# mLSTM value products turned round: values stationary, weights passing, transposed back one projection later

## The chip, the cores and the metric

The kernel runs on one core of a Trainium2 chip. The metric is the device time of one execution in microseconds (us), taken as the median of several runs. The core has these engines: PE (TensorE: matmuls, and PEld for its weight loads), DVE (VectorE), ACT (ScalarE), POOL (GpSimd) and SP (SyncE, which issues nearly all DMA transfers here). Each engine works through its own queue in order. PE writes its results to PSUM, in 8 banks of 128 partitions x 512 fp32 numbers.

## The reference

Two layers, each with a mixer (four pairs of mLSTM heads beside eight heads of neighbourhood attention) and an MLP, over 1024 latent tokens and 256 context tokens; all of it in fp32. The change concerns the mLSTM alone. For one direction of one head, the reference computes, chunk by chunk:

```python
s = jnp.einsum('bhtd,bhsd->bhts', qc, kc) * w_intra
num = w_prev[..., None] * jnp.einsum('bhtd,bhde->bhte', qc, C) + jnp.einsum('bhts,bhse->bhte', s, vc)
qn = w_prev * jnp.einsum('bhtd,bhd->bht', qc, n) + jnp.sum(s, axis=-1)
h = num / jnp.maximum(jnp.abs(qn), jnp.exp(-m_t))[..., None]
...
C = w_c[..., None, None] * C + jnp.einsum('bhs,bhsd,bhse->bhde', w_s, kc, vc)
n = w_c[..., None] * n + jnp.einsum('bhs,bhsd->bhd', w_s, kc)
```

and of both directions' results `head_layernorm(hx_f + hx_b, norm_g) * jax.nn.sigmoid(o)`, where `head_layernorm` takes away the mean over the 64 channels of a head and divides by their spread. The kernel works in chunks of 128 tokens instead of 64, and it gets the sums `qn` and `n` as one more channel, whose value is 1 for every token.

## The kernel before

Tokens: T = 1280, in ten chunks of 128; a tile is two chunks (`u` = 0, 1), so there are five tiles `i`, the first of them the context. Heads go by pairs `pr` = 0 to 3 with `h` = 0, 1 in a pair; directions are `s` = 0, 1. `HD` = 64 channels a head.

`mlstm_out` (L540) is the mLSTM output stage of a layer. Its steps run over `seq`, 20 pairs (pr, i). A step projects a tile (`project_j`, L418: for each `u` eight k-tiles of 128 with three fp32r matmuls each, `mm3`, L85, that stand for one fp32 product by a split into high and low parts), 512 columns wide: keys and values of the next pair `pr + 1` (or, at the last pair, attention values), and queries and gate of this pair. In layer 1 the context has no output (`need_ctx` is false), so tile 0 projects 256 columns and has no output tile; 16 tiles are left there, 20 in layer 0.

- `kv_take` (L474) rotates the keys (`rope`, L431) into `kt`, copies the values to `va` (in the tile `kva`, 65 numbers a head, the last set to 1 by POOL), and leaves room for the turned keys `kT`.
- `kv_turn` (L493) transposes `kt` on PE and copies it to `kT` on ACT.
- `kv_state` (L500) weighs the values by token into `vw` on DVE (L517), multiplies them by `kt` (L519: head h to partitions h*64 to h*64 + 63 of the output) and adds to the running forward state `cst` (L526); the backward part waits in `kvb` for `kv_back` (L528).
- `mlstm_tile` (L592) is a generator in five stages: (1) load `gb`, the gate sums, by DMA; gate `og` on ACT; rotated queries `qr`; and the weights `wt` = exp(min(gb + tab, mask)) (L620 on DVE, L621 on ACT); (2) transpose `qr` (L625) into `qT` (L627); (3) scores and old-state products into four banks `sb` (L636, L637); (4) P = scores x wt on DVE (L647), value products with P stationary and `va` passing, for each u, h and s (L649), old state weighed into `hh` (L652) and the sum (L653); then the normaliser `den`, and the layer norm (L657 to L675); (5) transpose back to channels (L679), copy `yT` and store.

`mlstm_out` interleaves these stages by hand: a tile's transposes and scores come after the next tile's projection has been issued, its values after that. A list scheduler then sets the order of each engine's queue, with the program's order as priority. It moves matmuls across the stages where data are ready. `tc.issue_after(x)` (in use at L201, L852 and L1488) puts the instructions of a block behind instruction x on its engine.

`tick` (L59) draws a piece of side work: first `fill` (in layer 0 a part of the modulation on PE, `ada`), and when that has run out and its argument is true, one row of `ada_rows` (L185; on DVE L202, one DMA of 512 KB each; 16 rows in this stage of layer 0). `project_j` ticks with true; a tile ticks with true for i = 2 and 4 (L629).

Weights: `joint_weights` (L536) loads four chunks of 128x1024 for a pair through `split_chunk` (L71): DMA to `wraw` (two buffers), ACT copies the high part to `whi` (L81), DVE takes the low part `wlo` (L82); four buffers each. `kv_weights` (L447) does the same for the first pair's keys, values and the gates in three chunks, outside this stage; in layer 0 `opening` (L1512, its order written out by hand) does it.

PSUM: `BANKS`, two of tag `mm` for projections and six of tag `q` for the rest.

## Time and profile before

| what | us |
|---|---|
| median of 3 runs | 2876.28 |
| lowest and highest run | 2873.52, 2878.64 |
| the profiled execution, its own time | 2880.66 |
| span of the profiled execution | 2878.9 |

The rows of the profile are shown in the prediction, where they are used. In a row of the timeline stand the start in us, the length in us, the engine (PE, PEld, DVE, ACT, POOL, SP), the line of the kernel, the operation, output<-inputs by the program's names, the shape and the count. Matmuls overlap: what one costs PE is the distance to the next start. In a row of groups stand after the bar the busy time, the mean of one in ns, and the idle time of the engine just before, with what ended it. An fp32 product (not fp32r) shows as two matmul records, two passes; a transpose as one. 576 records of L649 stand for 36 tiles of 8 value products.

### The profile page before, as it was taken

Reading aid. Unit: us, or ns where it says so; the run is one execution under the profiler, and the core shown is the slowest. Engines: PE = TensorE matmul, PEld = TensorE weight load, DVE = VectorE, ACT = ScalarE, POOL = GpSimd, SP = SyncE. Lnnn points to the kernel's source line nnn. Section 1 sums busy time; section 2 is a strip of 40 time slices with the busy share of each in tenths; the row PEclk is TensorE's granted clock in tenths of the full one; section 3 lists DMA queues with packets and bytes.
Section 4 is the critical chain, followed back from the end, with each engine's and each line's share of the span. In section 5 each row is a group of like instructions: output and inputs, shape, how many; then the busy total and the mean of one; then the engine's idle time right before and its main releaser. Section 6 shows DMA issues by size and latency. Waiting matters only on the chain. (4 is left out here: it accounts for less than half of the span.)

```text
span 2878.9 us, 45683 instructions
## 1 busy us (share of the span) xinstructions
PE 2832.6 (98%) x16644; PEld 2409.0 (84%) x16644; DVE 2210.9 (77%) x5097; ACT 1263.5 (44%) x2426; POOL 67.2 (2%) x117
## 2 busy tenths in 40 slices
PE   8999999999999999999999999999999999999998
PEld 5888888889888888888889988888887788888888
DVE  7789987776798777599877778877785887759774
ACT  5333335564553333344554333335564533334453
POOL 0000000010000000000000000000010000000000
PEclk9999999999999999999999999999999999999999
DMA  7533333236446556798977122213346354478673
GB/s 249 165 115 105 112 120 107 90 121 201 152 163 227 191 191 205 276 324 289 319 254 256 67 89 71 75 64 116 110 143 194 130 191 142 155 255 311 210 255 100
DMA packets 278946, 497.42 MB, mean 173 GB/s; under 512 B 23328, under 2 KB 119584, under 8 KB 278720
## 3 DMA queue, kind: packets, MB, share of 16 engines
q1 hardware_dynamic: 278720, 494.49, 51.3%
q8 instruction: 131, 2.15, 0.3%
q14 instruction: 95, 0.78, 0.1%
HBM read 398.82 MB, written 95.59 MB: 172 GB/s over the span
## 5 line engine op out<-in xcount | busy, mean ns | idle before, releaser
L87 PE MATMUL q<-ah,whi 128*128 128x512 f32 (+1 forms) x1472 | 548.9, 373 | 2.5 <-ACT ah L997 1.9
L89 PE MATMUL q<-ah,wlo 128*128 128x512 f32 (+1 forms) x1472 | 547.9, 372 | 1.2 <-DVE wlo L998 1.1
L88 PE MATMUL q<-al,whi 128*128 128x512 f32 (+1 forms) x1472 | 548.4, 373 | 0.0
L87 PE MATMUL mm<-ah,whi 128*128 128x512 f32 (+1 forms) x1120 | 387.5, 346 | 1.5 <-ACT whi L81 1.3
L89 PE MATMUL mm<-ah,wlo 128*128 128x512 f32 (+1 forms) x1120 | 386.3, 345 | 0.5 <-DVE wlo L82 0.5
L88 PE MATMUL mm<-al,whi 128*128 128x512 f32 (+1 forms) x1120 | 386.2, 345 | 0.0
L87 PEld LDWEIGHTS q<-ah,whi 128*128 128x128 f32 x1472 | 277.5, 189 | 52.3 <-ACT ah L997 2.7
L89 PEld LDWEIGHTS q<-ah,wlo 128*128 128x128 f32 x1472 | 277.7, 189 | 50.8 <-DVE wlo L998 2.3
L88 PEld LDWEIGHTS q<-al,whi 128*128 128x128 f32 x1472 | 277.8, 189 | 48.9 <-issue 1.4
L87 PE MATMUL mm<-whi,ah 128*128 128x512 f32 (+2 forms) x864 | 313.3, 364 | 0.9 <-DVE st L313 0.4
L88 PE MATMUL mm<-wlo,ah 128*128 128x512 f32 (+2 forms) x864 | 309.3, 359 | 0.6 <-DVE wlo L82 0.6
L89 PE MATMUL mm<-whi,al 128*128 128x512 f32 (+2 forms) x864 | 307.8, 357 | 0.0
L87 PEld LDWEIGHTS mm<-ah,whi 128*128 128x128 f32 x1120 | 212.7, 190 | 29.2 <-issue 2.0
L89 PEld LDWEIGHTS mm<-ah,wlo 128*128 128x128 f32 x1120 | 212.6, 190 | 26.3 <-DVE wlo L82 1.0
L88 PEld LDWEIGHTS mm<-al,whi 128*128 128x128 f32 x1120 | 212.9, 190 | 25.1 <-issue 0.2
L997 ACT CAST ah<-raw 128x512 fp32r<-128x512 f32 (+1 forms) x264 | 143.0, 566 | 123.4 <-PE q L89 63.8
L87 PEld LDWEIGHTS mm<-whi,ah 128*128 128x128 f32 x864 | 163.4, 189 | 28.6 <-issue 3.5
L89 PEld LDWEIGHTS mm<-whi,al 128*128 128x128 f32 x864 | 163.6, 189 | 23.0 <-issue 0.7
L88 PEld LDWEIGHTS mm<-wlo,ah 128*128 128x128 f32 x864 | 163.8, 190 | 22.6 <-DVE wlo L82 0.8
L998 DVE TENSOR_TENSOR al<-raw,ah 128x512 fp32r<-128x512 f32 (+1 forms) x264 | 158.3, 623 | 24.9 <-ACT ah L997 24.5
L998 DVE TENSOR_TENSOR wlo<-raw,whi 128x1024 fp32r<-128x1024 f32 x84 | 102.5, 1223 | 73.3 <-ACT whi L997 70.8
L82 DVE TENSOR_TENSOR wlo<-wraw,whi 128x1024 fp32r<-128x1024 f32 (+2 forms) x90 | 108.2, 1204 | 56.9 <-ACT whi L81 55.0
(290 smaller groups left out, 5286.3 us busy)
## 6 DMA issues: line engine op xcount, KB each, us to landing
raw<-w SPq DMA_DIRECT2D x168, 512.0 KB
raw<-hid SPq DMA_DIRECT2D x104, 512.0 KB
wada<-w_adaT SPq DMA_DIRECT2D x96, 512.0 KB
wraw<-w SPq DMA_DIRECT2D x80, 512.0 KB
hid<-hb SPq DMA_DIRECT2D x128, 256.0 KB
hid<-ht SPq DMA_DIRECT2D x96, 256.0 KB
gb<-gscr SPq DMA_DIRECT2D x36, 512.0 KB
wada<-w_ada SPq DMA_DIRECT2D x32, 512.0 KB
```

Source lines behind the costliest of these rows:

```text
L82: nc.vector.tensor_sub(lo[:, :n], raw[:, :n], fview(hi[:, :n]))
L87: mm(out, lh, rh, start=start, stop=False, skip_group_check=True)
L88: mm(out, lh, rl, start=False, stop=False, skip_group_check=True)
L89: mm(out, ll, rh, start=False, stop=stop, skip_group_check=True)
L997: ins = self.nc.scalar.copy(hi, src)
L998: self.nc.vector.tensor_sub(lo, src, fview(hi))
```

## The change

- **Values.** A value product is turned: the values of head h (128 tokens x 64) are stationary, and the weighed scores of both directions pass, 256 columns. Head 0 goes to the upper 64 partitions of a bank, head 1 to the lower. The result, channels by tokens, is copied to `nt` (ACT) and transposed back by four transposes; there is one `hh` of 512 columns a tile. `P` is gone: DVE multiplies the scores into `w`, which is also the tile that `gb` was loaded to.
- **64 columns instead of 65.** The normaliser takes the place of the last channel. `less_last` takes the last value channel's weights from those of the other 63 as the weights come in (on `wraw`, on DVE, for the value columns of pairs 0 to 3); the layer norm does not see such a shift, and the last channel's sum is then 0, which POOL writes.
- **Order.** A step is now: projection; then `gap` for the tile before: the transposes of queries, keys and results; state products and the value products of the tile before that one; scores; the transposes back; and on DVE the weighing, the norm, the old state. Each group of blocks is put behind the last PE instruction with `behind`. Weighing by token (`kv_weigh`) is a step ahead of `kv_state`. The second tick of a step is always with true.
- **Buffers.** `va`, `kT` and `vw` have tiles of their own; `value_store` stores each chunk by its own DMA.

```diff
+    def less_last(self, raw, n, c):
+        v = raw[:, :n].rearrange("p (k c) -> p k c", c=c)[:, :, 128:256].rearrange("p k (h e) -> p k h e", e=HD)
+        self.nc.vector.tensor_sub(v[:, :, :, 0:HD - 1], v[:, :, :, 0:HD - 1], v[:, :, :, HD - 1:HD].to_broadcast([128, n // c, 2, HD - 1]))
 ...
+    def kv_weigh(self, pr, i):
+        st, tab = self.mst[pr], self.gt[0]
+        if i == 0:
+            st["cst"] = self.mp.tile([128, NT, 2, 64], F32, name="cst", bufs=2)
+            self.nc.vector.memset(st["cst"][:, 0, 0, :], 0.0)
+            self.nc.vector.memset(st["cst"][:, 1, 1, :], 0.0)
+        st["vw"][i] = []
+        for u in range(2):
+            vw = self.mp.tile([128, 256], F32, name="vw", bufs=WV)[:].rearrange("p (s h e) -> p s h e", s=2, h=2)
+            ws = tab[:, 2 * i + u, 1, :, pr * 2:pr * 2 + 2].unsqueeze(3).to_broadcast([128, 2, 2, 64])
+            self.nc.vector.tensor_tensor(vw, st["va"][i][:, u, :, :].unsqueeze(1).to_broadcast([128, 2, 2, 64]), ws, ALU.mult)
+            st["vw"][i].append(vw)
 ...
+    def behind(self):
+        return self.tc.issue_after(next(i for i in reversed(self.nc.cur_bb.bb.instructions) if i.engine == mybir.EngineType.PE))
 ...
+        n2, skip = NT // 2, 0 if need_ctx else 1
+        seq = [(pr, i) for pr in range(4) for i in range(n2)]
+        groups = [[(pr, i) for i in range(o, min(o + GROUP, n2))] for pr in range(4) for o in range(skip, n2, GROUP)]
+        due = {seq.index(g[-1]) + 1: g for g in groups}
+        self.scored, self.turning, states, tiles = [], [], [], {}
+        Wq, keys = [], []
+        def gap(group):
+            now = [tiles.pop(t) for t in group]
+            with self.behind():
+                p = self.bank() if now or states else None
+                for z, t in enumerate(now):
+                    for u in range(2):
+                        self.nc.tensor.transpose(p[:, (2 * z + u) * 128:(2 * z + u + 1) * 128], t["qr"][:, u, :], self.ident)
+                spare = 2 - len(now)
+                held = [self.kv_turn(*s, p[:, (len(now) + z) * 256:(len(now) + z + 1) * 256]) for z, s in enumerate(states[:spare])]
+                if now:
+                    n = len(now) * 256
+                    qT = self.mb.tile([128, 256 * GROUP], F32, name="qT", bufs=2)
+                    self.nc.scalar.mul(qT[:, :n], p[:, :n], 0.125)
+                    for z, t in enumerate(now):
+                        t["qT"] = qT[:, z * 256:(z + 1) * 256].rearrange("p (u t) -> p u t", u=2)
+                for f in held:
+                    f()
+                for s in states[spare:]:
+                    self.kv_turn(*s)
+                self.mlstm_turn(l)
+            with self.behind():
+                for s in states:
+                    self.kv_state(*s)
+                    if s[1] == n2 - 1:
+                        self.kv_back(s[0])
+                states.clear()
+                for t in self.scored:
+                    self.mlstm_values(t)
+            with self.behind():
+                for t in now:
+                    self.mlstm_scores(t)
+            with self.behind():
+                for t in self.scored:
+                    self.mlstm_back(t)
+            for t in now:
+                self.mlstm_weigh(t)
+            for t in self.scored:
+                self.mlstm_norm(t)
+            for t in now:
+                self.mlstm_before(t)
+            self.scored = now
+            self.tick(True)
+        for n, (pr, i) in enumerate(seq):
             if n and i == 0:
                 W = self.joint_weights(l, pr)
+            mine = (pr, i) in [t for g in groups for t in g]
+            with self.behind():
+                accs = self.project_j(W, i, hi, lo, 512 if mine else 256)
             if pr < 3:
                 if i == 0:
                     self.kv_begin(pr + 1)
                 self.kv_take(pr + 1, i, accs)
             else:
                 self.value_store(l, 1, i, [a[:, 0:256].unsqueeze(1) for a in accs])
+            if mine:
+                tiles[pr, i] = self.mlstm_tile(l, pr, i, [a[:, 256:512].unsqueeze(1) for a in accs])
+            if n in due:
+                gap(due[n])
+            if pr < 3:
+                self.kv_weigh(pr + 1, i)
+                states.append((pr + 1, i))
+        Wq.extend(self.qk_weights(l, 0, which) for which in (1, 0))
+        with self.behind():
+            keys.append(self.qk_project(Wq[0], 0, hi, lo))
+        gap(due[len(seq)])
+        with self.behind():
+            keys.append(self.qk_project(Wq[0], 1, hi, lo))
+        gap([])
+        keys.append(self.qk_project(Wq[0], 2, hi, lo, "q"))
+        self.mlstm_turn(l)
+        return Wq, keys
 ...
+                    a, ws = pr * 2 + h, w[:, s, h, u * 128:(u + 1) * 128]
+                    nc.vector.scalar_tensor_tensor(ws, ws, tab[:, 2 * i + u, 0, s, a:a + 1], self.mask[:, s, :], ALU.add, ALU.min)
+            nc.scalar.activation(w[:, s], w[:, s], AF.Exp)
+        return dict(pr=pr, i=i, w=w, og=og, qr=qr)
 ...
+    def mlstm_scores(self, t):
+        mm, st, i = self.nc.tensor.matmul, self.mst[t["pr"]], t["i"]
+        t["S"] = [self.bank() for _ in range(2)]
+        for u in range(2):
+            for h in range(2):
+                hp, o = slice(h * 64, (h + 1) * 64), u * 256
+                mm(t["S"][h][:, o:o + 128], st["kT"][i][hp, u, :], t["qT"][hp, u, :], start=True, stop=True, skip_group_check=True)
+                mm(t["S"][h][:, o + 128:o + 256].rearrange("p (s e) -> p s e", s=2), t["qT"][hp, u, :],
+                   st["cst"][hp, 2 * i + u, :, :], start=True, stop=True, skip_group_check=True)
+    def mlstm_weigh(self, t):
+        for h in range(2):
+            S = t["S"][h][:].rearrange("p (u c) -> p u c", u=2)[:, :, 0:128]
+            ws = t["w"][:, :, h, :].rearrange("p s (u t) -> p s u t", u=2)
+            self.nc.vector.tensor_tensor(ws, S.unsqueeze(1).to_broadcast([128, 2, 2, 128]), ws, ALU.mult)
+    def mlstm_before(self, t):
+        hh = t["hh"] = self.mb.tile([128, 2, 2, 2, 64], F32, name="hh", bufs=2)
+        i, a = t["i"], t["pr"] * 2
+        for h in range(2):
+            qc = t["S"][h][:].rearrange("p (u c) -> p u c", u=2)[:, :, 128:256].rearrange("p u (s e) -> p u s e", s=2)
+            wp_ = self.gt[0][:, 2 * i:2 * i + 2, 2, :, a + h].unsqueeze(3).to_broadcast([128, 2, 2, 64])
+            self.nc.vector.tensor_tensor(hh[:, :, :, h, :], qc, wp_, ALU.mult)
+    def mlstm_values(self, t):
+        va = self.mst[t["pr"]]["va"][t["i"]]
         p = self.bank()
         for u in range(2):
             for h in range(2):
+                self.nc.tensor.matmul(p[h * 64:(h + 1) * 64, u * 256:(u + 1) * 256].rearrange("p (s t) -> p s t", s=2), va[:, u, h, :],
+                                      t["w"][:, :, h, u * 128:(u + 1) * 128], start=True, stop=True, skip_group_check=True)
+        t["nt"] = self.mb.tile([128, 512], F32, name="nt", bufs=GROUP)
+        self.nc.scalar.copy(t["nt"][:], p[:])
+    def mlstm_back(self, t):
+        t["num"] = self.bank()
+        for z in range(4):
+            self.nc.tensor.transpose(t["num"][:, z * 128:(z + 1) * 128], t["nt"][:, z * 128:(z + 1) * 128], self.ident)
-                nc.vector.tensor_tensor(P[:, :, h, :], sb[h][:, 0:128].unsqueeze(1).to_broadcast([128, 2, 128]), wt[:, u, :, h, :], ALU.mult)
-                for s in range(2):
-                    nc.tensor.matmul(n4[:, s, h, :], P[:, s, h, :], va[:, u, h, :], start=True, stop=True, skip_group_check=True)
 ...
+    def mlstm_norm(self, t):
+        nc, mp, tab, i, pr, hh = self.nc, self.mb, self.gt[0], t["i"], t["pr"], t["hh"]
+        hf = hh[:].rearrange("p u s h e -> p (u s h e)")
+        nc.vector.tensor_tensor(hf, hf, t["num"][:], ALU.add)
 ...
+    def mlstm_turn(self, l):
+        if not self.turning:
+            return
         p = self.bank()
+        for z, (_, _, hsf) in enumerate(self.turning):
+            for u in range(2):
+                self.nc.tensor.transpose(p[:, (2 * z + u) * 128:(2 * z + u + 1) * 128], hsf[:, u, :], self.ident)
+        yT = self.mb.tile([128, 256 * GROUP], F32, name="yT", bufs=2)
+        n = len(self.turning) * 256
+        self.nc.scalar.copy(yT[:, :n], p[:, :n])
+        for z, (pr, i, _) in enumerate(self.turning):
+            self.nc.sync.dma_start(self.yscr[l][pr * 128:(pr + 1) * 128, i * 256:(i + 1) * 256], yT[:, z * 256:(z + 1) * 256])
+        self.turning = []
 ...
+        views = [a[:, u, :] for a in accs for u in range(2 // len(accs))]
+        for u, a in enumerate(views):
+            v, c = self.mp.tile([128, 256], F32, name="va", bufs=VB), 2 * i + u
+            self.nc.scalar.copy(v[:], a)
+            self.nc.sync.dma_start(self.vscr[l][c * 128:(c + 1) * 128, z * 256:(z + 1) * 256], v[:])
 ...
-MB = 8
+VB = 10
+TB = 7
+WV = 6
+GROUP = 1
+GB = 4
+OB = 5
+QB = 3
```

The same `less_last` stands ahead of the splits in `opening`, and `joint_weights` asks for it for pairs 0 to 2 (whose chunks hold the values of pairs 1 to 3).

More of the change, by code (lines that the diff above doesn't have):

```diff
@@ L74, in split_chunk @@
         nc.sync.dma_start(raw[:, :n], src)
+        if values:
+            self.less_last(raw, n, values)
         return self.split_raw(raw, n)
+    def less_last(self, raw, n, c):
+        v = raw[:, :n].rearrange("p (k c) -> p k c", c=c)[:, :, 128:256].rearrange("p k (h e) -> p k h e", e=HD)
+        self.nc.vector.tensor_sub(v[:, :, :, 0:HD - 1], v[:, :, :, 0:HD - 1], v[:, :, :, HD - 1:HD].to_broadcast([128, n // c, 2, HD - 1]))
     def split_raw(self, raw, n):
@@ L465, in mlstm_kv @@
         for i in range(NT // 2):
+            self.kv_weigh(0, i)
             self.kv_state(0, i)
@@ L477, in kv_take @@
         kt = self.mp.tile([128, 2, 128], F32, name="kt", bufs=6)
-        kva = self.mp.tile([128, 516], F32, name="kva", bufs=MB)
+        va = self.mp.tile([128, 256], F32, name="va", bufs=VB)[:].rearrange("p (u h e) -> p u h e", u=2, h=2)
         acc = [a[:, :256].unsqueeze(1) for a in accs]
@@ L489, in kv_take, with kv_turn @@
         st["kts"].append(kt)
         st["va"].append(va)
-        st["kT"].append(kva[:, 260:516].rearrange("p (u t) -> p u t", u=2))
-    def kv_turn(self, pr, i):
+    def kv_turn(self, pr, i, p=None):
         nc, st = self.nc, self.mst[pr]
-        p = self.bank()
+        held, p = p is not None, p if p is not None else self.bank()[:, 0:256]
         for u in range(2):
             nc.tensor.transpose(p[:, u * 128:(u + 1) * 128], st["kts"][i][:, u, :], self.ident)
-        nc.scalar.copy(st["kT"][i].rearrange("p u t -> p (u t)"), p[:, 0:256])
+        kT = self.mp.tile([128, 256], F32, name="kT", bufs=TB)
+        st["kT"].append(kT[:].rearrange("p (u t) -> p u t", u=2))
+        copy = lambda: nc.scalar.copy(kT[:], p)
+        return copy if held else copy()
@@ L511, in kv_state @@
         for u in range(2):
[L512 to L517 removed]
             for h in range(2):
[L519 removed]
+                nc.tensor.matmul(p4[h * 64:(h + 1) * 64, u, :, :], st["kts"][i][:, u, h * 64:(h + 1) * 64], st["vw"][i][u][:, :, h, :],
@@ L1577, in opening @@
         steps(rest, 1)
+        for z in range(2):
+            self.less_last(raws[z], chunks[z][1], 288)
         W = [self.split_raw(raws[z], chunks[z][1]) for z in range(2)]
@@ L1589, in opening @@
         scale(2, r2, range(6, 8))
+        self.less_last(raws[2], chunks[2][1], 288)
         W.append(self.split_raw(raws[2], chunks[2][1]))
```

136 lines of the change are left out of this document (21 added, 115 removed).

## The prediction

> **What bounds the kernel now.** I read the page first, then busy time by stretches, then the timeline of TensorE (PE) over one step of the stage that the change rewrites, then the groups and the waits of that stage.
>
> ```profile
> span 2878.9 us, 45683 instructions
> PE 2832.6 (98%) x16644; PEld 2409.0 (84%) x16644; DVE 2210.9 (77%) x5097; ACT 1263.5 (44%) x2426; POOL 67.2 (2%) x117
> 130.63:439.13 308.50, 307.85 (x1914) 255.43 (x1912) 266.07 (x1022) 102.38 (x277) 16.33 (x35) 1.00 0.34 114
> 1681.71:1950.00 268.29, 265.35 (x1655) 224.39 (x1654) 210.16 (x823) 88.49 (x235) 12.78 (x29) 1.00 0.20 66
> ```
>
> The last two lines are the mLSTM output stage of layer 0 and of layer 1: stretch, length, then busy PE, weight loads, DVE, ACT, POOL, the granted clock, the DMA share and GB/s. PE is never idle, at full clock, for 577 of 2879 us. So what counts is how many microseconds of issue PE has there. Matmuls overlap, so a matmul costs the distance to the next start, not its duration. One step of layer 0 (20 steps there, 16 in layer 1 with a tile of their own), in starts and lengths:
>
> ```profile
> 241.93 1.89 PE L649 MATMUL q<-kva,P 128*128 128x65 f32 x16
> 243.63 0.48 PE L87 MATMUL mm<-whi,ah 128*128 128x512 f32 x1
> 243.94 0.39 PE L88 MATMUL mm<-wlo,ah 128*128 128x512 f32 x1
> ...
> 245.79 0.38 PE L625 MATMUL q<-consts,qr 128*128 128x128 f32 x2
> ...
> 246.54 0.67 PE L519 MATMUL q<-vw,kt 128*64 128x130 f32 x8
> 247.13 0.50 PE L636 MATMUL q<-qT,kva 64*128 64x128 f32 x4
> ...
> 248.33 0.50 PE L87 MATMUL mm<-whi,ah 128*128 128x512 f32 x1
> 248.67 0.39 PE L88 MATMUL mm<-wlo,ah 128*128 128x512 f32 x1
> 248.90 0.40 PE L89 MATMUL mm<-whi,al 128*128 128x512 f32 x1
> ...
> 257.31 1.89 PE L649 MATMUL q<-kva,P 128*128 128x65 f32 x16
> ```
>
> From 241.93 to 257.31 a step is 15.38 us. Of these the 48 projection products (L87 to L89) take 48 x 0.227 = 10.9 us (248.67 to 248.90 is such a distance). The value products (L649), 16 passes for 8 fp32 products, take 241.93 to 243.63 = 1.70; six transposes 245.79 to 246.54 = 0.75; the state products (L519) 0.59; scores and old-state products (L636, L637) 247.13 to 248.33 = 1.20. Two projections just behind other kinds are late: 243.63 to 243.94 is 0.31 and 248.33 to 248.67 is 0.34, against 0.23. Sum 10.9 + 1.70 + 0.75 + 0.59 + 1.20 + 0.08 + 0.11 = 15.33, the step to 0.05.
>
> **Part 1: the value products.** Before, P (128 columns) is loaded for each of 8 products, and only 65 columns pass behind it: 1.70 / 16 = 0.106 us a pass. After, the values (128x64) are loaded and 256 columns of weights pass, for head 0 to the upper half of the output partitions and for head 1 to the lower: 4 products, 8 passes. The neighbourhood attention already does this form with 128 columns, and one fp32 form passes 256:
>
> ```profile
> 518.13 0.66 PE L947 MATMUL q<-pc,vc 128*64 128x128 f32 x8
> 518.62 0.82 PE L947 MATMUL q<-pl,vt 128*64 128x128 f32 x12
> 519.27 0.61 PE L947 MATMUL q<-pc,vc 128*64 128x128 f32 x8
> L947 PE MATMUL q<-pc,vc x576: 270/273/324, 466.5 to 2162.4; 128*64 128x128 f32 x192
> L1421 PE MATMUL q<-tmp,ones x16: 378/379/483, 2849.6 to 2870.5; 128*128 128x256 f32 x16
> ```
>
> Twelve passes take 518.62 to 519.27 = 0.65 us, 0.054 each, or 0.108 for a pair: the two heads run beside each other. 256 columns make a pass 379 - 273 = 106 ns longer, so a pair costs about 0.215, and four pairs 0.86 us. Bounds: 0.86 if they pair as here, 8 x 0.215 = 1.72 if they don't. I take 0.86, since L947 and L519 have the same shape of weights and the same halves.
>
> Here the Trainium skill speaks against the change: TensorE: Matmul & The Clock Gate, Part 3, "The mechanism", says that weight loads overlap running matmuls only when the row group differs. Column halves share their rows, so by it the loads of the values would stand exposed. It is a rival below.
>
> **Part 2: transposed back.** Four new 128x128 transposes a tile, behind the scores, and the next projection behind them instead of behind the scores:
>
> ```profile
> 279.10 0.44 PE L497 MATMUL q<-consts,kt 128*128 128x128 f32 x2
> 279.30 0.48 PE L87 MATMUL mm<-whi,ah 128*128 128x512 f32 x1
> 280.01 0.67 PE L519 MATMUL q<-vw,kt 128*64 128x130 f32 x8 [0.23 <-DVE bs L667]
> 384.88 0.38 PE L679 MATMUL q<-consts,hs 128*128 128x128 f32 x2
> 385.02 0.48 PE L88 MATMUL mm<-wlo,ah 128*128 128x512 f32 x1
> 385.33 0.40 PE L89 MATMUL mm<-whi,al 128*128 128x512 f32 x1
> ```
>
> Two transposes between projections take 0.14, two behind the scores 0.20, so the first costs 0.06 more. Six in a row cost 0.75 with the step to the next kind, so a further one 0.11. Four: 0.20 + 2 x 0.11 = 0.42. The projection behind them is 0.31 against 0.23: 0.08. The changes of kind from transposes to column halves and from these to scores stay as many; that the state products now stand beside the value products saves none.
>
> Sum for PE per tile: away 1.70 + 0.08 + 0.11 = 1.89; added 0.86 + 0.42 + 0.08 = 1.36; **0.53 us less**. With 36 tiles, 19 us. 65 to 64 columns for the state and the scores I cost at nothing, since these passes start some 0.1 us apart as transposes of 128 columns do.
>
> **Part 3: DVE.** Groups of the layer 0 stage (count, then busy, mean ns, idle before):
>
> ```profile
> L647 DVE TENSOR_TENSOR P<-q,wt 128x256 f32<-128x256 f32 x80 | 31.4, 414 | 2.0 <-PE q L637 2.0
> L652 DVE TENSOR_TENSOR hh<-q,tab 128x130 f32<-128x130 f32 x80 | 20.6, 284 | 0.0
> L202 DVE CUSTOM_DVE_ANT_0 wada<-wada,consts 128x1024 f32<-128x1024 f32 x16 | 20.3, 1269 | 0.3 <-DMA wada<-w_adaT 0.2
> L653 DVE TENSOR_TENSOR hh<-hh,q 128x260 f32<-128x260 f32 x40 | 16.9, 423 | 13.6 <-PE q L649 13.2
> L660 DVE TENSOR_TENSOR hh<-hh,den 128x512 f32<-128x512 f32 x20 | 13.7, 686 | 0.3
> L517 DVE TENSOR_TENSOR vw<-kva,tab 128x260 f32<-128x260 f32 x30 | 12.2, 416 | 0.5 <-POOL kva L488 0.5
> 226.53:303.90 77.37, 77.14 (x471) 64.60 (x470) 72.14 (x271) 25.95 (x72) 4.22 (x10) 1.00 0.33 111
> ```
>
> Per tile away: 4 x 0.414 + 4 x 0.284 + 2 x 0.423 = 3.64. Added: weighing 2 x 512 elements, old state 2 x 256, one sum of 512: 2 x 0.686 + 2 x 0.414 + 0.686 = 2.89. 0.75 less. Against this, less_last adds 252 elements to each of the four weight chunks, priced by the 260 of L517: 1.7 us at the borders to pairs 1 and 2. And the modulation rows (L202) are moved: now two ticks a step may take one where before some 1.4 did, so 16 rows are done in 8 steps instead of 11. Five steps (last line) now have 72.1 us of DVE and 7 rows; after, with 10, 72.1 - 3.7 + 1.7 + 3 x 1.35 = 74.2, against PE's 77.4 - 5 x 0.53 - 0.5 = 74.2. So DVE stands level with PE for 8 steps and is free later. PE loses nothing if DVE never runs dry in these steps, and 8 x 0.05 x 15 = 6 us if DVE idles in 5% of each (7% now: 77.4 - 72.1). I take **+2**, nearer to nothing, since a tile's weighing and norm are now due a step later.
>
> **Other queues.** POOL gets a memset of 4 elements a tile (it is busy 16 of 308 us), ACT the copy of nt. On SP the value stores become two of half the size (20 to 40), and the load of gb now fills w itself, held over two steps in one of 4 buffers. DMA is at 0.34 and 0.20 in the two stages, so I cost these at nothing; if a load of w came late, DVE and then Part 5's copies would carry it.
>
> **Part 4: borders and opening.** 279.30 to 280.01 is a projection 0.48 late, because the last state product of a pair waits for DVE. The waits view counts this wait twice in layer 0 (130 to 450 us) and three times in layer 1 (1660 to 1960 us; total, times, longest):
>
> ```profile
> PE q L519 <- DVE bs L667: 0.5, 2, 0.2
> ...
> PE q L519 <- DVE bs L667: 1.9, 3, 0.8
> L82 DVE TENSOR_TENSOR wlo<-wraw,whi 128x1024 fp32r<-128x1024 f32 x16 | 19.3, 1208 | 2.4 <-ACT whi L81 2.1
> 32.40 0.68 DVE L173 COPY arow<-mm 64x512 f32<-64x512 f32 x1 [0.17 <-PE mm L151]
> ```
>
> That product is now weighed a step ahead, so the wait goes: 2 x 0.48 + 1.9 = 2.9 us. What is late next is the last weight chunk: raw DMA, less_last (0.42), ACT, DVE (L82). PE reaches it earlier now, most of all in layer 1, where the first projection of a pair has 256 columns. From nothing to 1.5 us at each of 6 borders, so 0 to 9; I take 2.9, half a microsecond a border, about the length of less_last, which gives back what went: **0** net, from -3 to +6. In the opening less_last stands between raw and split; DVE reaches the copy at 32.40 with 0.17 to spare, and two pieces of 378 elements (0.6 each by L517) come before: 0 to 1.0, **+0.7**.
>
> **Part 5: the order.** Before, the scheduler put nine projections between a tile's rope and its transposes (243.63 to 245.79). After, blocks are pinned on PE: projection, transposes, state and values, scores, transposes back. Scores need the ACT copies qT and kT, made while PE does state and values (1.45 us); the transposes back need nt (512 wide, some 0.6 us of ACT) in the 1.2 us of scores. Behind a late copy stands all of PE.
>
> ```profile
> ACT wt L621 <- DVE wt L620: 35.0, 22, 4.3
> PEld q L636 <- ACT kva L498: 2.1, 12, 0.2
> L611 ACT ACTIVATE og<-og 128x256 f32<-128x256 f32 x20 | 8.3, 417 | 0.6
> ```
>
> Before, scores waited 0.2 us at most for a copy. But now the transposes come right at the end of a projection, where ACT also has the next tile's gate (two of L611's kind and two smaller), and an Exp at the head of ACT's queue can wait up to 4.3 us for DVE. Bounds per step: 0, and 1.0 (two gate operations of 0.42 and a scrap). I take 0.17, what half a gate operation costs: 36 x 0.17 = **+6**.
>
> The sum is -19 + 2 + 0 + 0.7 + 6 = -10.3 us. The profiled execution took 2880.66 (span 2878.9 and 1.8 around it), so 2870.4 for it. It lies 4.4 above the median of the runs, 2876.28; so the median goes to **2866 us**.
>
> **The rivals.** *Copies show in full*: 0.5 us a step, as if a whole gate operation stood ahead of each copy. Then 36 x 0.5 = 18 stands against 19 + 0, with 2.7 from the rest: 2878, no change. For it: ACT waits for DVE in its queue already. Against: one tile's lag is a whole step now, and ACT is 33% busy. *Copies stand behind the Exp of the weights* (slower): if ACT's order puts these, which wait for DVE, ahead of qT or nt at each step, PE waits some 1.0 us a step, +36; 2876 - 19 + 36 + 3 = 2896. It decides from 0.53 us a step. *The halves don't run beside each other at 256 columns*: +0.86 x 36 = 31, 2866 + 31 = 2897. Against it stand the twelve passes in 0.65 us. *The loads of the values stand exposed*: 0.134 us (the weight load of this shape) for each of four pairs is 0.54 a tile, 19 in all: 2885.
>
> ```profile
> L947 PEld LDWEIGHTS q<-pc,vc x576: 132/137/139, 466.5 to 2162.3; 128*64 128x64 f32 x192
> ```
>
> L947's pairs, 0.108 us apart, hold no room for an exposed load of 0.134. The Trainium skill's rule on row groups would make this rival true; by that spacing the trace disagrees with it for column halves.
>
> **The numbers.** Forecast (a gain of 6 to 24) 0.68; copies in full 0.18; slower by copies 0.11; by halves 0.02; by loads 0.01. This kernel can be told from no change at about 0.2%, 5.8 us. Low end: no ACT wait, borders at -3, no DVE lag: 2876 - 19 - 3 = 2854. High end: the copies in full with the borders at +4: 2882. Faster 0.68, same 0.18, slower 0.14.
>
> **What would show it.** Right: in a layer 0 step without L202's neighbours, eight value passes in 0.85 to 1.0 us right behind the state products, four transposes in 0.42 behind the scores, and a step of 14.8 to 15.0. Wrong: starts of scores or back transposes with idle time that ends on ACT; a border step over 17 us; DVE over 97% busy between the sixth and fourteenth step while PE is idle.

## The result and the profile after

| | before | after |
|---|---|---|
| median (range) of 4 runs each | 2876.58 us (2873.52 to 2878.64) | 2904.75 us (2898.99 to 2908.02) |
| ratio | | 1.0097, 95% interval 1.0076 to 1.0117 |
| profiled execution | 2880.66 us | 2902.07 us |

The change makes the kernel slower by about 28 us; the forecast was 10 us faster. The busy times on the page of the changed kernel, the cores view of before, and that of after:

```profile
PE 2825.2 (97%) x16500; PEld 2383.2 (82%) x16500; DVE 2205.7 (76%) x4947; ACT 1267.6 (44%) x2472; POOL 70.4 (2%) x153
```

```profile
core 0: 2878.9 us, clock 0.996
```

```profile
core 0: 2900.3 us, clock 0.992
```

PE has 7 us less of busy time and DVE 5, and yet the span is 21.4 us longer: PE is idle more, and its mean clock is lower. A plain step of layer 0 in the timeline of PE after (start, length, idle time and releaser in brackets where there is any):

```profile
227.12 0.38 PE L573 MATMUL q<-consts,qr 128*128 128x128 f32 x2
...
228.36 1.03 PE L699 MATMUL q<-w,va 128*64 128x256 f32 x8
229.32 0.50 PE L673 MATMUL q<-qT,kT 64*128 64x128 f32 x4
...
230.52 0.66 PE L708 MATMUL q<-consts,nt 128*128 128x128 f32 x4
230.93 0.48 PE L94 MATMUL mm<-whi,ah 128*128 128x512 f32 x1
...
241.94 0.38 PE L573 MATMUL q<-consts,qr 128*128 128x128 f32 x2
```

The value products (L699) take 228.36 to 229.32 = 0.96 us where they took 1.70, the four transposes back (L708) 230.52 to 230.93 = 0.41, and the step 14.82 in place of 15.38. The four pairs of value passes start 0.21 us apart (228.36, 228.58, 228.79, 229.01), as computed; the rest of the 0.96 is the change to the scores. So the steps do what was forecast, and the loss must lie elsewhere. Cutting both traces at the first pass of each stage shows where (us; the last two lines of a stage are parts of it, cut at the end of its last 512-column projection):

| stretch | before | after | difference |
|---|---|---|---|
| start to the first projection | 36.67 | 39.31 | +2.6 |
| from there to the state passes of pair 0, layer 0 | 80.56 | 80.33 | -0.2 |
| state passes of pair 0, layer 0 | 2.38 | 5.90 | +3.5 |
| output stage, layer 0 | 325.09 | 329.94 | +4.8 |
| - its steps | 305.4 | 296.4 | -9.1 |
| - its end | 19.7 | 33.6 | +13.9 |
| from there to the state passes, layer 1 | 1213.69 | 1214.21 | +0.5 |
| state passes of pair 0, layer 1 | 2.39 | 5.50 | +3.1 |
| output stage, layer 1 | 288.23 | 294.54 | +6.3 |
| - its steps | 268.5 | 261.9 | -6.6 |
| - its end | 19.7 | 32.7 | +13.0 |
| from there to PE's last pass | 921.49 | 921.97 | +0.5 |

The steps gain 15.7 us together. The two ends lose 26.9, the state passes of pair 0 6.6, the opening 2.6. (The other 0.2 of the 21.4 us lies behind PE's last pass.) The waits of PE over the whole of after, and the two rows of before that answer to the second and third of them (us in total, times, longest):

```profile
PE q L747 <- DVE hs L737: 20.4, 8, 5.6
...
PE q L532 <- DVE vw L521: 4.7, 4, 1.3
...
PE mm L183 <- DVE arow L180: 2.3, 1, 2.3
...
PE q L708 <- ACT nt L702: 1.9, 3, 0.7
```

```profile
PE q L519 <- DVE bs L667: 2.3, 5, 0.8
...
PE mm L176 <- DVE arow L173: 0.9, 1, 0.9
```

The largest, 20.4 us, is the output transposes (L747, mlstm_turn) waiting for the normed tile; next are the state passes (L532) waiting for weighed values. The copy of nt, a copy that the forecast feared, costs 1.9 in all.

**The end of a stage.** PE, then DVE, of layer 0 after:

```profile
428.00 0.38 PE L573 MATMUL q<-consts,qr 128*128 128x128 f32 x2
433.99 0.66 PE L747 MATMUL q<-consts,hs 128*128 128x128 f32 x2 [5.61 <-DVE hs L737]
434.58 1.98 PE L699 MATMUL q<-w,va 128*64 128x256 f32 x8
436.49 0.81 PE L673 MATMUL q<-qT,kT 64*128 64x128 f32 x4
```

```profile
425.84 0.68 DVE L714 TENSOR_TENSOR hh<-hh,q 128x512 f32<-128x512 f32 x1
...
427.26 1.22 DVE L89 TENSOR_TENSOR wlo<-wraw,whi 128x1024 fp32r<-128x1024 f32 x1
...
428.51 1.17 DVE L89 TENSOR_TENSOR wlo<-wraw,whi 128x1024 fp32r<-128x1024 f32 x1
...
433.42 0.42 DVE L737 TENSOR_TENSOR hs<-hs,og 128x256 f32<-128x256 f32 x1
```

Normalizing a tile takes DVE from 425.84 to 433.84, 8 us, two splits of the next weights (2.4 us) among it. In a plain step 11 us of projection lie between the transposes back and the output transposes behind them. At the end only the 24 short products of qk_project(0) lie there, from 425.05 to 428.00. PE stands 5.6 us in the pinned order, though the operands of the value products and scores behind it are there: DVE had weighed w by 425.93, ACT had copied qT by 428.80. Then it runs slowly: eight value passes take 434.58 to 436.49 = 1.91 us in place of 0.96. The two ends as stretches of the windows view, from their first key projection on (columns as in the prediction's stretches: length, busy PE, weight loads, DVE, ACT, POOL, granted clock, DMA share, GB/s):

```profile
425.05:455.48 30.43, 22.86 (x123) 17.64 (x122) 19.11 (x67) 5.21 (x14) 0.11 (x1) 0.83 0.16 54
...
1940.09:1969.72 29.63, 21.72 (x123) 16.60 (x122) 19.19 (x67) 5.78 (x14) 0.11 (x1) 0.88 0.17 60
```

Of the 26.9 us that the ends lose, 15.5 are idle time of PE (30.43 - 22.86 and 29.63 - 21.72). The lower clock costs at most 0.17 x 30.43 + 0.12 x 29.63 = 8.7 more. What is left is work that was put off and that the cut therefore counts to the end.

**State passes of pair 0**, PE after:

```profile
119.64 1.53 PE L532 MATMUL q<-vw,kt 128*64 128x128 f32 x24
122.20 0.44 PE L532 MATMUL q<-vw,kt 128*64 128x128 f32 x4 [1.03 <-DVE vw L521]
123.87 1.75 PE L532 MATMUL q<-vw,kt 128*64 128x128 f32 x12 [1.22 <-DVE vw L521]
```

Twenty-four passes, six weighed tiles, run through; the seventh tile waits. Six is WV. The old kernel had eight buffers of vw and put the last two tiles into ropea, ten in all for pair 0's ten tiles, which can be weighed before any state pass runs.

**The opening**, DVE and then PE after:

```profile
21.84 1.01 DVE L82 TENSOR_TENSOR wraw<-wraw 128x378 f32<-128x378 f32 x2
23.36 2.03 DVE L89 TENSOR_TENSOR wlo<-wraw,whi 128x864 fp32r<-128x864 f32 x2 [0.52 <-ACT whi L88]
...
33.73 0.68 DVE L180 COPY arow<-mm 64x512 f32<-64x512 f32 x1
```

```profile
34.56 0.43 PE L183 MATMUL mm<-consts,arow 64*128 64x64 f32 x4 [2.31 <-DVE arow L180]
34.92 4.47 PE L158 MATMUL mm<-wada,silu 128*32 128x512 f32 x12
39.31 0.40 PE L94 MATMUL q<-whi,ah 128*128 128x288 f32 x1
```

The two subtractions (1.01 us) and DVE's wait for the split that they hold up (0.52) put the copy of arow at 33.73 in place of 32.40. PE waits 2.31 in place of 0.9, and of the twelve passes behind it, which start two at a time, the slow ones are 0.84 us apart where 0.42 is usual: 4.39 us in place of 3.08.

### The profile page after: what moved, and what is told of

It is laid out like the page before. It is cut to its first block, busy times and chain, and to the rows that moved or that the text cites. A ratio compares the mean times of both kernels' runs of the same rounds, so it can differ in the third digit from the quotient of the medians.

```text
span 2900.3 us, 45396 instructions
## 1 busy us (share of the span) xinstructions
PE 2825.2 (97%) x16500; PEld 2383.2 (82%) x16500; DVE 2205.7 (76%) x4947; ACT 1267.6 (44%) x2472; POOL 70.4 (2%) x153
## 4 chain that ended last, share of the span: by engine, by line
PE 73%; DVE 12%; issue 6%; DMA 5%; ACT 2%; SPq 1%; DVEq 0%; POOL 0%; ACTq 0%; POOLq 0%
PE q L94 13%; PE q L96 13%; PE q L95 13%; PE mm L94 9%; PE mm L95 9%; PE mm L96 9%; PE q L1017 1%; DVE wlo L89 1%; PE q L699 1%; DMA raw<-hid 1%; DMA S<-rpbt 1%; PE q L673 1%; DMA w<-gscr 1%; PE q L965 1%; PE q L983 1%
## 5 line engine op out<-in xcount | busy, mean ns | idle before, releaser
L1068 DVE TENSOR_TENSOR al<-raw,ah 128x512 fp32r<-128x512 f32 (+1 forms) x264 | 158.0, 622 | 26.9 <-ACT ah L1067 26.7
L94 PE MATMUL q<-th,whi 128*128 128x512 f32 x384 | 150.3, 391 | 2.1 <-DVE s L1232 2.0
```

The lines of the kernel that those rows point to most:

```text
L94: mm(out, lh, rh, start=start, stop=False, skip_group_check=True)
L1068: self.nc.vector.tensor_sub(lo, src, fview(hi))
```

## The experiments

The theory: the turned products gain what was forecast, and the loss is waits at three places where a late operand has too little PE work or too few buffers ahead of it, with slow passes behind each long wait. Rivals: DVE is simply a step behind and a mended wait only moves; or the subtraction on the weights (less_last) or the pinned order costs throughout. Ratios are to the kernel before as it ran beside each experiment; the changed kernel has 1.0097. The median of the kernel before moved between 2876.58 and 2880.43 us from one set of runs to the next, so two experiments of different sets are compared by their ratios (0.001 is 2.9 us), and a difference inside their intervals is not told from noise.

**Ten buffers for pair 0**

```diff
-            vw = self.mp.tile([128, 256], F32, name="vw", bufs=WV)[:].rearrange(...)
+            tag = ("ropea", 2) if pr == 0 and i == 4 else ("kT", TB) if pr == 0 and i == 3 else ("vw", WV)
+            vw = self.mp.tile([128, 256], F32, name=tag[0], bufs=tag[1])[:].rearrange(...)
```

> Against the changed kernel (2904.75 us, ratio to the kernel before 1.0097). The weighed values of pair 0 get ten buffers in place of six (two of the tag ropea and two spare ones of kT are borrowed). Theory A (too few buffers): in the 40 state passes of pair 0, the two gaps of 1.3 and 1.5 us of each layer are waits for VectorE, which itself waits for a passed buffer; with ten buffers the block falls from 5.9 and 5.5 us to about 2.4, and the time by about 6.5 us to 2898, ratio 1.0075. Rival B (VectorE is late there by its own queue, whatever the buffers): the two gaps stay within 0.3 us each, and the time moves by under 1 us. Nothing else should move under either.

2897.83 us, ratio 1.0063 (1.0048 to 1.0078). PE in the same place:

```profile
119.17 1.53 PE L533 MATMUL q<-vw,kt 128*64 128x128 f32 x24
120.53 0.61 PE L533 MATMUL q<-kT,kt 128*64 128x128 f32 x8
120.97 0.61 PE L533 MATMUL q<-ropea,kt 128*64 128x128 f32 x8
121.50 0.50 PE L94 MATMUL mm<-whi,ah 128*128 128x512 f32 x1
```

The block takes 2.33 us in both layers, as before the change. Theory A holds: the two blocks give back 3.57 and 3.17 us, 6.7 together. The ratio falls by 0.0034, some 10 us, which agrees within the intervals.

**Output transposes in the last block of a gap**

```diff
-                self.mlstm_turn(l)
             with self.behind():
                 for s in states:
...
                     self.mlstm_back(t)
+                self.mlstm_turn(l)
```

> Against the changed kernel (2904.75 us, 1.0097). The transposes of the normed outputs go from the first block of a gap to the last, behind the back transposes. Theory A (the position of these transposes in the pinned TensorE order holds up everything behind them): the waits of 5.6 and 5.9 us at the end of the two stages and of 1.9, 1.9 and 3.4 us at the borders of layer 1 (18.6 us together) go for the most part, as do the passes at half speed behind them; the time falls by 12 to 20 us to about 2889, ratio 1.0043. Rival B (VectorE is a whole step late there): what it does next, the weights times the scores, is then the wait; the value passes or the copy of their result take over the idle time, and the time falls by 4 us or less.

2892.97 us, ratio 1.0040 (1.0027 to 1.0054): 0.0057 less, some 16 us, in the middle of what theory A gave. The gaps at the borders of layer 1 fall from 5.59, 5.59 and 7.11 us to 3.80 each. At the end of each stage a wait of 3.6 us stays, now behind the scores:

```profile
PE q L747 <- DVE den L718: 7.2, 2, 3.6
```

So rival B is right for a part of it: at the end the wait moves and shrinks from 5.6 to 3.6 us.

**Without less_last; less_last on GpSimd**

```diff
     def less_last(self, raw, n, c):
+        return
```

> Against the changed kernel (2904.75 us, 1.0097). Leaves out the subtraction of the last value column of each head from the other 63 in the weights, everywhere (24 on the joint weights, 6 on the others), so the values are not lessened. Theory A (these subtractions stand ahead of the splitting copies on VectorE and hold up the weights): the first projection of layer 0 starts 2.4 us earlier, the borders of layer 1 lose the wait of 3.5 us of ScalarE on the raw weights, those of layer 0 come to 11.0 us a projection in place of 12.5 to 12.8; 8 us less in all (5 to 12), about 2897, ratio 1.0069. Rival B (the borders are late by the transfers of the weights, not by the subtraction): the opening gains its 2.4 us, the borders nothing; about 2902, ratio 1.0089.

```diff
-        self.nc.vector.tensor_sub(v[:, :, :, 0:HD - 1], ...
+        self.nc.gpsimd.tensor_sub(v[:, :, :, 0:HD - 1], ...
```

> Against the changed kernel (2904.75 us, 1.0097). The same subtractions done by GpSimd in place of VectorE. Theory A (what costs is the place in VectorE's queue): nearly all that leaving them out gives is gained, about 6 us, to 2899. Rival B (what costs is the extra link between the transfer of the weights and their splitting, whoever does it): GpSimd takes at least as long over one, and the gain is under 2 us, or it is a loss of up to 5 us.

Without it 2904.17 us, ratio 1.0079 (1.0063 to 1.0094); on GpSimd 2906.13, 1.0094 (1.0075 to 1.0113). Neither is told from the changed kernel by its time; the traces tell more. Without it the first projection starts at 37.97 and the wait for arow is 0.9 again. The last two borders of layer 0 fall from 12.52 and 12.77 us of projection to 11.00 and 11.65; the weights that come in at a stage's third border, to pair 3, are not lessened in any kernel, so that the second figure is not the subtraction's own (it is 12.75 on GpSimd). But those of layer 1 get longer, 14.9 us in place of 13.2 at the first. PE there without less_last:

```profile
1741.56 0.38 PE L574 MATMUL q<-consts,qr 128*128 128x128 f32 x2
...
1745.29 0.41 PE L748 MATMUL q<-consts,hs 128*128 128x128 f32 x2 [3.13 <-DVE hs L738]
1745.63 0.66 PE L533 MATMUL q<-vw,kt 128*64 128x128 f32 x8
1746.12 1.41 PE L700 MATMUL q<-w,va 128*64 128x256 f32 x8
```

The projection takes 6.2 us in place of 7.6, so PE is 1.4 us earlier at the output transposes, whose operand comes no sooner (9.9 us after the border's first pass, 9.8 before), so the wait for the weights is added to the other: one of 3.1 us, with slow passes behind it, in place of three of 0.2, 0.8 and 1.6 with none. Neither theory foresaw that; what the borders of layer 1 wait for in the end is the norm, and the waits for the weights only took up part of that time. On GpSimd the same shows: the projections at these borders take 6.23, 6.38 and 6.22 us, and the gaps behind them 9.06, 7.12 and 8.73 in place of 5.59, 5.59 and 7.11. So the time is rival B's of that run, but its reason, the extra link whoever does it, is not what these borders show.

**The end of the stage reordered**: two key projections ahead of the first closing gap, the third ahead of the second, a query projection ahead of the last output transposes. (One more line, not shown, lets the first pair of the attention use that projection.)

```diff
+        with self.behind():
+            keys.append(self.qk_project(Wq[0], 1, hi, lo))
         gap(due[len(seq)])
         with self.behind():
-            keys.append(self.qk_project(Wq[0], 1, hi, lo))
-        gap([])
-        keys.append(self.qk_project(Wq[0], 2, hi, lo, "q"))
+            keys.append(self.qk_project(Wq[0], 2, hi, lo, "q"))
+        gap([])
+        with self.behind():
+            keys.append(self.qk_project(Wq[1], skip, hi, lo, "q"))
         self.mlstm_turn(l)
```

> Against the changed kernel (2904.75 us, 1.0097). Only the third edit: the order of the key projections, gaps and first query projection at the end of each stage. Theory A (between the last two gaps lie 2.95 us of projection where elsewhere there lie 11, and whatever VectorE and ScalarE have then to do is waited for): with 8.5 us before the first gap its wait of 5.9 us falls to about 1, the waits of 1.7 and 1.1 us behind it and the half-speed passes go; 9 us per stage, about 2888, ratio 1.004. Rival B (the wait is a transfer or a buffer that comes when it comes): under 5 us in all.

2902.83 us, ratio 1.0084 (1.0071 to 1.0098). In layer 0 the first wait falls from 5.9 to 0.4 us (from start to start, beyond the usual distance), as A says, but starts with 1.64 and 1.07 us missing follow as before, then 3.2 at the last output transposes and a row of passes 0.427 us apart. In layer 1 the wait goes on to the next stage's first projection (3.0 us, for DVE's work on the keys, L804). By size this is rival B's. In layer 0 B's reason, a transfer or buffer, is not what the trace shows: it is the same norm, one gap later.

**All three together**

> Against the changed kernel (2904.75 us, ratio 1.0097) and the kernel before. Three edits together: ten buffers for the weighed values of pair 0 (alone: the two blocks came to 2.3 us, ratio 1.0063), the output transposes in the last block (alone: ratio 1.0040), and at the end of a stage two key projections ahead of the first of the two closing gaps, the third ahead of the second, and the first query projection ahead of the last output transposes. Theory A (the loss sits in those places, and the saving of about 0.54 us a tile is real): the gains add, and the waits of 3.9 and 1.1 us with the half-speed passes behind them that the second edit left at each stage's end go too; 2904.75 - 8 - 14 - 12 gives about 2871 (2866 to 2877), ratio 0.997, faster than the kernel before. Rival B (the waits at the end are VectorE a step behind and only move): about 2884, ratio 1.001 to 1.003.

2881.80 us, ratio 1.0014 (1.0005 to 1.0023): 24 of the 28 us are back by the ratios, but not the 34 that A had. Rival B's number; the wait of the last tile's norm, 2.7 us, stays at the end of layer 0's stage, and 3.0 us at layer 1's, for DVE's work on the keys of the next stage.

**The transposes back made twice**

```diff
-        for z in range(4):
+        for z in (0, 1, 2, 3, 0, 1, 2, 3):
```

> Against the changed kernel's profiled run (2902 us). The four transposes back of each tile are made twice into the same bank (36 tiles, 0.41 us of TensorE a tile). Theory A (TensorE sets the pace of the steps, so the 0.54 us a tile that the change takes off it are gained in full): a plain step goes from 14.84 to 15.25 us and the time rises by 12 to 15 us. Rival B (VectorE or ScalarE set the pace of the changed steps, which would put the saving where it can't be seen): the step grows by less than 0.15 us, the time by under 5 us.

2915.48 us in one run, and a profiled span of 2913.7, 13.4 above the changed kernel's. Three plain steps in a row, first after, then with the doubled transposes (columns as in the prediction's stretches):

```profile
227.12:271.59 44.47, 44.47 (x271) 36.10 (x270) 43.08 (x153) 14.51 (x47) 2.64 (x9) 1.00 0.32 110
```

```profile
229.23:274.95 45.72, 45.72 (x283) 37.41 (x282) 43.58 (x154) 15.11 (x46) 2.64 (x9) 1.00 0.35 113
```

1.25 us more in three steps, 0.42 a step: in these steps all of it shows, as theory A has it. PE sets their pace though DVE is busy for 97% of them, and what the change takes off PE there is a real gain. Over the whole kernel one run says less: the two stages grew by 4.7 and 10.9 us, where 20 and 16 tiles would give 8.3 and 6.7.

**The order left to the planner**

```diff
-        return self.tc.issue_after(next(i for i in reversed(...) if i.engine == mybir.EngineType.PE))
+        return contextlib.nullcontext()
```

> Against the changed kernel (2904.75 us, 1.0097). The written order of the TensorE blocks (each block of a gap behind the one before) is left to the planner, which spreads the small passes between the projection's. Theory A (the pinned order makes each late operand hold up all that stands behind it): waits at the ends of the stages and at the state passes of pair 0 shrink by 10 us or so, but each extra change between kinds of passes costs about 0.1 us, at two to four more a step 8 to 14 us; the sum lies between 2896 and 2912, the plain step at 15.0 to 15.4 us. Rival B (the pinned order costs nothing): plain step within 0.1 of 14.84 us and the same waits.

2893.43 us, ratio 1.0053 (1.0038 to 1.0069). The plain step stays at 14.8 us, as B says, and the output transposes' waits shrink from 20.4 to 13.4 us, as A says: each is half right, and with nothing lost in the steps the time falls below the 2896 to 2912 that A gave. The waits that go are those at the borders of layer 1. At the end of layer 0 the planner puts the second key projection ahead of the late output transposes by itself, but 6.7 us of wait are left in the gap after.

**Further at the end, then GpSimd, then the free order.** The first kernel has the first two edits and a stage's end in this order: key projections 0 and 1, gap, key projection 2, value products, first query projection, transposes back and output transposes, second query projection, last output transposes. The second adds less_last on GpSimd, the third instead leaves the order to the planner.

> Against the kernel before, and the run with the three edits together (ratio 1.0014), whose two stage ends still held waits of 1.1, 2.7 and 3.0 us and some ten passes at half speed. The same, with the end stretched further: the first query projection lies between the last value products and their transposes back, the second between those and the last output transposes. Theory A (every late operand at the end lacks projection work ahead of it, and 3 to 5.5 us more of it suffices): the waits at the two ends fall under 1 us each and the half-speed passes go; 5 us a stage, about 2872, ratio 0.998 (0.997 to 0.999): the turned products with their surroundings mended beat the kernel before. Rival B (VectorE has more to do at the end than lies ahead of it, the lessening of operands for the next stage too): the wait goes on to the next stage's first passes, and the ratio stays at 1.000 to 1.0015.

> The run above with the subtractions of the last value column on GpSimd. Alone this gave nothing (1.0094 against 1.0097), since the transposes of the normed outputs then waited longer at the borders of layer 1 (projection 7.6 to 6.2 us, but 3.8 more in the gap). Theory A (with those transposes out of the way the time that the weights come earlier is kept): borders 1.5 us shorter, six of them, ratio 0.995 to 0.997. Rival B (the borders are set by the splitting of the weights and the transfers): within 0.001 of the run above.

> The first run of this call with the written order of the TensorE blocks left to the planner. Alone that gave 1.0053 in place of 1.0097, with the plain step still at 14.8 us. Theory A (what it gained alone were waits of output transposes and at the end, which are gone here): within 0.001 of the first run. Rival B (the written order costs in other places too): 0.002 or more below it.

| | median | ratio to before |
|---|---|---|
| end stretched | 2880.64 | 1.0005 (0.9996 to 1.0014) |
| the same, less_last on GpSimd | 2874.18 | 0.9985 (0.9976 to 0.9994) |
| end stretched, order free | 2878.79 | 1.0005 (0.9996 to 1.0014) |

In the first, the last output transposes no longer wait, but PE behind them does:

```profile
447.92 0.41 PE L759 MATMUL q<-consts,hs 128*128 128x128 f32 x2
451.32 0.79 PE L94 MATMUL mm<-ah,whi 128*128 128x512 f32 x1 [2.99 <-DVE nk L813]
```

Its rival B holds: DVE reads the key projections only once the norm is done, and the next projection needs their bank. With that the wait has left the stage and not gone. On GpSimd the subtraction now pays, as theory A of that run said, but by less than its 0.995 to 0.997: with the output transposes out of the way the 256-column projections at the first two borders of layer 1 fall from 7.92 to 6.29 us and the gaps behind them stay at 3.80. Those are two borders of the six that A counted on, 3.3 us of the 7.4 between the two profiled spans (the third has no subtraction). Another 3.4 lie between the two stages; that they are the subtraction's is not shown, since that stretch came to 1212.9 to 1216.1 us in kernels that are alike there. This version is the fastest, 3 to 4 us below the kernel before (0.15%). The free order gives nothing more, as its theory A has it.

## Why the prediction was wrong

- **The step that failed is the one from the plain step to all 36 tiles.** The sum has no term for the end of a stage and none for the state passes of pair 0. Part 3 took it as help that "a tile's weighing and norm are now due a step later", and the rivals that "one tile's lag is a whole step now". Between two plain steps that holds, since 11 us of projection lie there. At the end of a stage the lag has to be paid out: 8 us of DVE stand against 2.95 us of projection, and PE waits in the pinned order. That cost 26.9 us where the sum has nothing. Ten weighed tiles in six buffers, which the last lines of the diff show, cost 6.6 more.
- **Part 4 names the wrong thing as late next** at most places: the last weight chunk, at six borders. At the first border of layer 0 nothing was late. At the other two that chunk was, but at 1.5 and 1.8 us (12.52 and 12.77 in place of 11.0), the upper bound and not the half microsecond taken, and the second of them without a less_last in its weights. At those of layer 1 the norm decides. In the opening the subtraction was priced well (1.01 us), but not the wait for the split behind it nor the slow passes: +2.6 for +0.7.
- **Parts 1 and 2 were right.** Value products 0.86 forecast, 0.96 measured with the change to the scores; transposes back 0.42 and 0.41; step 14.85 (15.38 - 0.53) and 14.82. The rivals on halves and on exposed loads fall by this: four pairs with their loads fit in 0.96 us. The Trainium skill, TensorE: Matmul & The Clock Gate, Part 3, "The mechanism", has loads overlap running matmuls only where the row group differs (beside a background weight buffer that it names as another way); for column halves this trace disagrees with the rule on row groups, at 0.24 us a pair. Doubling the transposes shows that the gain counts. One reading was loose: PE "is never idle" in the two stages leaves out 0.65 and 2.94 us of idle time in the rows shown.
- **Part 3 (+2) was too dear.** DVE is busy for 43.08 of 44.47 us in the busiest steps, level with PE as computed, and PE has no idle time there.
- **Part 5 (+6) and the rivals built on it were wrong in kind.** "Behind a late copy stands all of PE" was right about the pinned order and wrong about the operand: copies late behind ACT cost 1.9 us in all (nt) and at most 0.1 for qT and kT, the normed tile 20.4. The rival that ended slower named the wrong engine and the wrong place.

The sum as measured: steps -15.7, ends +26.9, state passes +6.6, opening +2.6, the rest +0.8: 21.2 of the 21.4 us of span. All the signs that the prediction named for being right came up, and the time still went the other way, since they were all about plain steps. Of the signs for being wrong, back transposes with idle time that ends on ACT came up three times, at 0.5 us in one step and 0.7 at each end. The others did not: border steps of layer 0 came to 16.3 and 16.6 us, under 17, and PE had no idle time where DVE was fullest. None of them pointed at the ends.

**Open**: the steps save some 0.54 us a tile, 19 us in all, and the fastest version keeps 3 to 4 of them. Its trace shows waits of 3.0 and 3.7 us on DVE's keys and 2.4 us in the opening, but the rest is not accounted for. A version that frees the banks of the keys earlier wasn't tried. That the rest of the opening's delay without less_last (37.97 against 36.67) is transfers that came later in that execution is argued from one profile (a wait of 3.1 for wada in place of 2.2).

## What to carry to other kernels

Where work is put off by one step, price the last steps first: find the longest chain on another engine between two blocks (8 us of DVE here), and look for the place where least of the bounding engine's work lies between them (2.95 us). Count the tiles alive at once against the buffers, ahead of a stage's steps too. A wait removed on a pinned engine pays only if the next operand in the order is ready; otherwise two short waits can become a longer one that costs more.

## What the hardware showed that was not expected

PE runs at half speed for a while after some idle times: passes of 512 columns start 0.427 us apart there, against 0.227. Which idle times, the windows view of after shows, cut where the granted clock changes (columns as above; busy PE is the second number, the clock stands behind POOL):

```profile
31.62:35.03 3.41, 1.10 (x10) 0.43 (x8) 2.80 (x6) 0.00 (x0) 0.00 (x0) 1.00 0.94 305
35.03:38.44 3.41, 3.41 (x10) 0.76 (x10) 2.31 (x9) 2.84 (x7) 0.00 (x0) 0.50 1.02 376
120.36:123.77 3.41, 1.25 (x20) 0.77 (x16) 3.41 (x8) 1.15 (x5) 0.00 (x0) 1.00 1.08 362
123.77:127.19 3.42, 3.32 (x16) 2.24 (x17) 3.29 (x17) 0.53 (x2) 0.00 (x0) 0.50 1.05 394
427.56:430.97 3.41, 0.82 (x8) 0.58 (x6) 3.27 (x6) 0.38 (x1) 0.00 (x0) 1.00 0.40 141
430.97:437.80 6.83, 3.81 (x21) 2.38 (x23) 2.23 (x13) 1.46 (x4) 0.11 (x1) 0.50 0.31 103
...
1881.64:1885.05 3.41, 1.62 (x18) 1.12 (x18) 1.89 (x9) 1.44 (x5) 0.11 (x1) 1.00 0.26 91
```

In this trace the half clock comes in stretches of 3.41 us or of twice that, all on one grid of 3.41 us. Before each of the three shown here PE had been busy for 0.82 to 1.25 us of such a stretch. So two gaps of 1.03 and 1.22 us close together, in the state passes of pair 0, had slow passes behind them (twelve state passes, 0.26 us a pair in place of 0.11, and three projections). A single gap of 3.1 us at a border of layer 1 (1880.3 to 1883.4) had none: it falls across two such stretches, and in the second, the last row, PE was still busy for 1.62 us. The clock stayed full behind that one, but was halved behind one with 1.68 us (444.63 to 448.04), so the runs do not give a sharp limit.

The Trainium skill, TensorE: Matmul & The Clock Gate, Part 1, "What's actually happening", says that the clock halves after an idle window of about 3.4 us. The half speed (0.427 us) and the length of the stretches (3.41 us) agree; a wholly idle window was not needed here, with 1.10 and 1.25 us of busy PE in it.

So a wait of PE can cost more than the waits view counts: over the whole span the mean clock fell from 0.9964 to 0.9915, at most 0.0049 x 2900 = 14 us.
